# A decoder trunk's opening and closing: gains carried by the first activation tile, casts in transfer order, first unit by tiles, last add in halves

## The chip, the core and the metric

One core of a Trainium2 chip runs the kernel alone. The metric is the device time of one execution in microseconds. A kernel's time is the median of several executions; beside it stands one profiled execution with its own time, whose trace gives the rows shown here. TensorE multiplies matrices, VectorE (DVE) and ScalarE (ACT) do elementwise work, GpSimd (POOL) does some more of it, and SyncE (SP) issues most transfers. Each of these has a queue of instructions that it works through in order.

## The reference

Two decoder layers over a residual stream of 256 rows by 2048 columns in float32. Layer 0 uses differential attention, layer 1 latent attention; each layer then attends into 256 memory rows and applies a squared-ReLU MLP of 8192 hidden columns. Every step is normed first, and one norm closes the trunk.

```python
def rms_norm(x, g):
    xf = x.astype(jnp.float32)
    y = xf * lax.rsqrt(jnp.mean(xf * xf, axis=-1, keepdims=True) + EPS)
    return (y * g.astype(jnp.float32)).astype(x.dtype)
...
    for i in range(DEPTH):
        h = rms_norm(x, attn_norm[i])
        x = x + attention(h)            # differential, then latent
        x = x + memory_cross_attention(rms_norm(x, cross_norm[i]), mem_h, ...)
        x = x + sq_relu_mlp(rms_norm(x, mlp_norm[i]), mlp_wup[i], mlp_wdown[i])
    return rms_norm(x, final_norm)
```

(The attention branches are drawn together into one call here.)

## The kernel before, in words

**Products in three passes.** TensorE works on numbers split in two: a value is cast to a short form (the high half), and what is lost by that is kept as a second number (the low half). A product of activation and weight is high x high, high x low and low x high, three matmuls of 512 columns each. So every weight tile is first cast by ScalarE (`whi`, line 193) and the rest is taken by VectorE (`wlo`, line 194). Activations that come from memory are split in `given_unit`: ScalarE multiplies a tile by its gain column (line 315), VectorE makes the low half (line 316).

**Units.** A *unit* is 512 rows of the inner dimension, four tiles of 128 (`k` = 0 to 3). Its weights for a chunk of 512 output columns are 128 x 2048 numbers, 1024 KB, in a buffer of the pool `wraw`, of which there are seven (`RAWS`); the activations of a unit as they arrive take such a buffer too. A buffer is given out again once its last reader is done. The halves of the weights lie in `whalf`, two tiles of the four for each unit. `matmul_chunk` runs over the four units of a chunk; for each unit over two halves of the weights (`h`), and in each half it goes through both row tiles (`t` = 0, 1, of 128 rows): `unit_part` then does two tiles `k` with three matmuls each. So a unit is 2 x 2 x 2 x 3 = 24 matmuls.

**Orders.** TensorE's instructions stay in the order in which the program writes them. The loads are kept in their written order on their queue (`load`, line 165). The order of the other engines' instructions comes from a planner that simulates the program when it is built.

**The opening (lines 903 to 922).** ScalarE's queue issues the first unit's weights in four pieces of 512 columns (one for each `k`), then loads its function table. TensorE runs 13 matmuls on a blank tile (`WARM`, line 913). SP's queue issues activation tile 0, the gain columns of all norms (`g`, 61 KB), tile 1, tiles 2 and 3 together, and then for units 1 and 2 the activations in two loads and the weights in two loads, for unit 3 the activations. The norm's row factors come later, from `x` itself; they are multiplied in after the products. `gsub` (line 979) is made from `g` for the end of the first attention.

**The closing (lines 1306 to 1328).** In the last chunk the second row tile's products follow the first's (`turns=True`). When a row tile's last 512 columns are done, VectorE adds them to the residual (`add_residual`, line 439), ScalarE squares and sums them (`sum_squares`, line 322), VectorE and GpSimd make the row factor, and ScalarE and VectorE scale the four pieces of 512 columns, which SP sends out in four transfers of 256 KB. The other pieces were added, squared and multiplied by the gain before.

Of the kernel before, what the change touches and what calls it, by code (L numbers as in the profile page):

```python
# [10 lines left out]
F32 = mybir.dt.float32  # L11
# [6 lines left out]
P = 128  # L18
D = 2048
# [4 lines left out]
WARM = 13  # L24
# [21 lines left out]
def trunk(ctx, tc, x, xT, mem, memT, positions, gcols, gfinal, lam_vecs, consts, W, out):  # L46
# [194 lines left out]
    def matmul_chunk(acts, width=CH, turns=False):  # L241
# [60 lines left out]
    def given_unit(src, u, gcol, pieces=None):  # L302


        dst = Held(unit())
        rows = raw_tile().rearrange("p (k t) -> p k t", t=S)
        for k, n in ((0, 1), (1, 1), (2, 2)) if pieces else ((0, 2), (2, 2)):
            load(rows[:, k : k + n], src[:, 4 * u + k : 4 * u + k + n, :])
            if pieces and k == 0:
                load(g, gcols)  # L310
            for i in range(k, k + n):
                if pieces:
                    pieces.next()
                raw, hi, gain = rows[:, i], dst[:, 0, i], g[:, gcol + 4 * u + i : gcol + 4 * u + i + 1]
                nc.scalar.activation(hi, raw, AF.Copy, scale=gain)  # L315
                nc.vector.scalar_tensor_tensor(dst[:, 1, i], raw, gain, f32(hi), ALU.mult, ALU.subtract)
        return dst

# [583 lines left out]

    first = raw_tile()
    for i in range(4):
        load(first[:, i * CH : (i + 1) * CH], W["da_wqkv"][0][:, i * CH : (i + 1) * CH], nc.scalar)
# [8 lines left out]
    acts = []  # L914
    norm = Stream(G_ATTN)
    pieces = split_pieces(first, 4 * CH, 4)
    ready.append(pieces.halves)
    for u in range(4):
        acts.append(given_unit(xT, u, G_ATTN, pieces if u == 0 else None))
        if 0 < u < 3:  # L920
            ready.append(split_weights(W["da_wqkv"][u], CH, loads=2))
            plan.pop(0)
    posf = keep.tile([P, NT], F32, name="posf")
# [149 lines left out]
    def mlp(l, norm, gnext):  # L1073
# [25 lines left out]
        def finish_chunk(of, ps, nxt):  # L1099
            for t in range(NT):  # L1100
                if of.kind == "up":
                    r = work.tile([P, CH], F32, tag="ev", name=nm("ev"), bufs=EVS)
                    out(*of.halves[0], t, ps[t], r, T_SQ)
                else:
# [203 lines left out]
    ss = [small.tile([P, 4], F32, tag="ss", name=nm("ss"), bufs=6) for _ in range(NT)]  # L1308

    def finish(c, t, ps):  # L1310
        cc = slice(c * CH, (c + 1) * CH)
        sum_squares(ss[t][:, c : c + 1], xs[t][:, cc])
        if c < 3:
            nc.gpsimd.tensor_tensor(xs[t][:, cc], xs[t][:, cc], gf[:, cc], ALU.mult)
            return
        r = row_norm(ss[t], D)
        for i in (3, 0, 1, 2):
            cc = slice(i * CH, (i + 1) * CH)
            y = xs[t][:, cc]
            if i == 3:  # L1320
                nc.vector.scalar_tensor_tensor(y, y, r[:, 0:1], gf[:, cc], ALU.mult, ALU.mult)
            elif i == 2:
                nc.vector.tensor_scalar(y, y, r[:, 0:1], None, ALU.mult)
            else:
                nc.scalar.activation(y, y, AF.Copy, scale=r[:, 0:1])
            nc.sync.dma_start(out[t * P : (t + 1) * P, cc], y)

    down(finish)


# [17 lines left out]
def _layout(i):  # L1348
# [9 lines left out]
    gains = [f["attn_norm"], f["cross_norm"], f["mlp_norm"], f["mem_norm"], f["mla_q_norm"], f["mla_kv_norm"], f["da_subln"]]  # L1358
# [57 lines left out]
```

## Time and profile before

| | |
|---|---|
| median of 3 runs | 2242.32 us (2242.08 to 2243.92) |
| the profiled execution | 2240.69 us |
| its span | 2238.9 us |
| TensorE busy | 2222.1 us, 99% |
| VectorE busy | 1736.5 us, 78% |
| ScalarE busy | 1363.5 us, 61% |
| moved by transfers | 454.72 MB, 203 GB/s over the span |

The span runs from the first to the last event of the trace; the 1.8 us between it and the execution's time lie around it. In a row of the timeline stand the start, the time it took, the engine, the line, the operation, what it writes and reads, the count (xN, where neighbours were drawn together), and in brackets the engine's idle time ahead of it with what ended it. In a table of windows each engine's busy time is followed by the count of its instructions; then come the clock that was granted to TensorE as a share of full speed, the share of the 16 DMA engines that was busy, and GB/s. `SPq` and `ACTq` are the queues' own rows, for the issue of a transfer.

### The profile page before, as it was taken

What the parts mean: (1) busy time and instruction counts of PE and PEld (TensorE: products, weight loads), DVE (VectorE), ACT (ScalarE), POOL (GpSimd) and SP (SyncE); (2) the same over time, 40 slices, a digit from 0 to 9 for tenths busy, and PEclk for the clock granted to TensorE, in tenths of its full rate; (3) what the DMA queues carried; (4) which work ended last, traced back from release to release, by engine and by line L of the source; (5) the groups of instructions that cost most, each with busy time, mean ns of one, the idle gap of its engine ahead of it and who ended that gap; (6) DMA issues with size and microseconds to landing.
All of it is one profiled execution on the core that took longest, in us unless ns stands there. A gap on an engine that the chain in (4) does not pass through costs nothing.

```text
span 2238.9 us, 27408 instructions
## 1 busy us (share of the span) xinstructions
PE 2222.1 (99%) x10521; PEld 1854.8 (83%) x10521; DVE 1736.5 (78%) x1892; ACT 1363.5 (61%) x1815; POOL 129.5 (6%) x222
## 2 busy tenths in 40 slices
PE   9999999999999999999999999999999999999998
PEld 7888888888888888888889888888888888888886
DVE  6655647679889889889865766778988988998974
ACT  6544645666666666666655755566766666665664
POOL 0210110000000000000000311000000000000001
PEclk9999999999999999999999999999999999999999
DMA  9446555435765766775845244634677677677681
GB/s 380 162 144 208 190 194 210 157 132 195 241 216 212 250 220 210 243 223 209 260 169 186 99 142 159 254 132 138 214 255 222 200 255 226 202 249 227 201 281 57
DMA packets 69683, 454.72 MB, mean 203 GB/s; under 512 B 7984, under 2 KB 8368, under 8 KB 17584
## 3 DMA queue, kind: packets, MB, share of 16 engines
q1 hardware_dynamic: 64944, 422.56, 52.4%
q0 software_dynamic: 4032, 29.36, 7.2%
q8 instruction: 82, 1.34, 0.2%
q10 hardware_dynamic: 576, 1.05, 0.2%
q14 instruction: 49, 0.40, 0.0%
HBM read 450.84 MB, written 2.10 MB: 202 GB/s over the span
## 4 chain that ended last, share of the span: by engine, by line
PE 89%; DVE 7%; DMA 2%; issue 1%; ACT 1%; ACTq 0%; POOLq 0%; DVEq 0%
PE mm L155 62%; PE pr L155 21%; DVE wlo L194 4%; PE ax L155 3%; PE ax L159 2%; DMA raw<-in_mlp_wup_dram 1%; PE mm L159 1%; DVE raw L748 1%; DVE unit L386 1%; ACT whi L193 0%; DVE raw L413 0%; DVE x L439 0%; DVE p L800 0%; DMA raw<-in_da_wqkv_dram 0%; DVE raw L397 0%
## 5 line engine op out<-in xcount | busy, mean ns | idle before, releaser
L193 ACT CAST whi<-raw 128x1024 fp32r<-128x1024 f32 (+2 forms) x962 | 1001.5, 1042 | 731.8 <-PE mm L155 593.6
L155 PE MATMUL mm<-whi,unit 128*128 128x512 f32 (+3 forms) x4544 | 1439.1, 389 | 2.3 <-ACT unit L315 1.3
L194 DVE TENSOR_TENSOR wlo<-raw,whi 128x1024 fp32r<-128x1024 f32 (+2 forms) x962 | 1145.0, 1209 | 371.2 <-ACT whi L193 359.5
L155 PEld LDWEIGHTS mm<-whi,unit 128*128 128x128 f32 x4544 | 849.8, 188 | 169.3 <-ACT unit L315 2.5
L155 PE MATMUL mm<-wlo,unit 128*128 128x512 f32 (+3 forms) x2272 | 876.4, 386 | 1.5 <-DVE wlo L194 1.5
L155 PE MATMUL pr<-whi,unit 128*128 128x512 f32 x1568 | 505.6, 391 | 0.0
L155 PEld LDWEIGHTS mm<-wlo,unit 128*128 128x128 f32 x2272 | 427.7, 188 | 81.7 <-DVE wlo L194 2.7
L155 PEld LDWEIGHTS pr<-whi,unit 128*128 128x128 f32 x1568 | 294.4, 188 | 60.8
L155 PE MATMUL pr<-wlo,unit 128*128 128x512 f32 x784 | 305.9, 390 | 1.7 <-DVE wlo L194 1.4
L748 DVE TENSOR_TENSOR raw<-raw,raw 128x2048 f32<-128x2048 f32 x84 | 192.1, 2287 | 33.8 <-DMA raw<-in_mlp_wup_dram 33.5
L155 PEld LDWEIGHTS pr<-wlo,unit 128*128 128x128 f32 x784 | 147.3, 188 | 34.1 <-DVE wlo L194 4.2
L439 DVE TENSOR_TENSOR x<-x,mm 128x512 f32<-128x512 f32 x152 | 100.8, 680 | 17.8 <-PE mm L155 17.3
L740 POOL DMA_DIRECT2D raw<-in_mlp_wup_dram x28 | 24.8, 885 | 1104.7 <-DVE wlo L194 1060.1
L288 ACT CAST unit<-ax 128x512 fp32r<-128x512 f32 (+1 forms) x88 | 48.8, 566 | 28.7 <-PE ax L159 26.2
L328 POOL TENSOR_TENSOR rs<-rs,mhalf 128x1 f32<-128x1 f32 (+1 forms) x28 | 23.6, 846 | 700.0 <-DVE rs L327 700.0
L289 DVE TENSOR_TENSOR unit<-ax,unit 128x512 fp32r<-128x512 f32 (+1 forms) x88 | 57.2, 658 | 3.2 <-ACT unit L288 2.4
L501 ACT ACTIVATE p<-ax,nmax 128x256 f32<-128x256 f32 (+1 forms) x80 | 33.7, 429 | 30.0 <-DVE nmax L499 29.4
L800 DVE TENSOR_TENSOR p<-pr,p 128x512 f32<-128x512 f32 x70 | 47.7, 682 | 0.8 <-PE pr L155 0.8
L1089 ACT ACTIVATE p<-p,r 128x512 f32<-128x512 f32 x56 | 40.5, 723 | 11.2 <-DVE p L800 10.8
L159 PE MATMUL ax<-identr,p 128*128 128x128 f32 x304 | 45.5, 272 | 0.0
L159 PEld LDWEIGHTS ax<-identr,p 128*128 128x128 f32 x304 | 37.4, 139 | 9.3
L322 ACT ACTIVATE junk<-x 128x512 bf16<-128x512 f32 x56 | 35.2, 628 | 9.4 <-DVE x L439 8.4
(135 smaller groups left out, 913.6 us busy)
## 6 DMA issues: line engine op xcount, KB each, us to landing
raw<-in_mlp_wup_dram SPq DMA_DIRECT2D x128, 1024.0 KB, 5.0
raw<-in_mlp_wdown_dram SPq DMA_DIRECT2D x128, 1024.0 KB, 5.1
raw<-in_da_wqkv_dram SPq DMA_DIRECT2D x45, 1024.0 KB, 5.1
raw<-in_mlp_wup_dram POOLq DMA_DIRECT2D x28, 1024.0 KB, 8.8
raw<-in_da_wo_dram SPq DMA_DIRECT2D x16, 1024.0 KB, 4.9
raw<-in_ca_wkv_dram SPq DMA_DIRECT2D x16, 1024.0 KB, 5.0
raw<-in_mla_wo_dram SPq DMA_DIRECT2D x16, 1024.0 KB, 5.9
raw<-in_ca_wq_dram SPq DMA_DIRECT2D x8, 1024.0 KB, 6.4
```

Source lines behind the costliest of these rows:

```text
L155: return nc.tensor.matmul(o, stationary, moving, start=start, stop=stop)
L159: nc.tensor.transpose(o, src, ident)
L193: nc.scalar.copy(hi, r)
L194: nc.vector.tensor_tensor(lo, r, f32(hi), ALU.subtract)
L288: nc.scalar.copy(hi, src)
L289: nc.vector.tensor_tensor(dst[:, 1, :n, t * P : (t + 1) * P], src, f32(hi), ALU.subtract)
L322: nc.scalar.activation(junk[:, : src.shape[1]], src, AF.Square, accum_out=acc)
L439: nc.vector.tensor_tensor(xc, xc, ps, ALU.add)
L501: nc.scalar.activation(pr[:, i * w : (i + 1) * w], sb[:, i * w : (i + 1) * w], AF.Exp, bias=nmax[:, i : i + 1], accum_out=ssum[:, i : i + 1],)
L748: nc.vector.tensor_tensor(o, o, q, ALU.add)
L800: nc.vector.tensor_tensor(o, p, q, op)
L1089: nc.scalar.activation(r, src, AF.Relu, scale=rstd[t])
```

## The change

- **Gains with the first tile.** A new input `xT0` holds the 16 gain columns of the first norm and activation tile 0 side by side. It goes into a buffer `ahead` of the pool `wraw`, which then takes the other three tiles of unit 0 too; units 1 to 3 read their gains from it (`first_gain`). The load of all gains `g` moves from second place on SP's queue to behind unit 1's loads.
- **Transfers.** ScalarE's queue issues weight pieces 0 and 1 only; pieces 2 and 3 go to SP's queue behind tiles 0 and 1, and tiles 2 and 3 follow them. For units 1 and 2 each half of the weights is now loaded ahead of the activations that go with it.
- **Casts in written order.** ScalarE and VectorE keep the written order through the opening: for unit 0 piece and tile in turn, for units 1 and 2 two tiles, then half of the weights.
- **First unit by tiles.** In the first chunk unit 0 takes each `k` through both row tiles before the next `k`. 13 blank matmuls become 9.
- **Closing.** The last piece of a row tile is added and squared in halves of 256 columns, with five partial sums in place of four. The sum is scaled in place. The pieces go out in the order 3, 0, 2, 1, piece 1 from ScalarE's queue.

```diff
-WARM = 13
+WARM = 9
...
+                if by_k and u == 0:
+                    for k in range(2):
+                        at = slice(k * width, (k + 1) * width)
+                        for t in range(NT):
+                            ah, al = acts[0].get(0, 2 * h + k, t), acts[0].get(1, 2 * h + k, t)
+                            mm3(ps[t][:, :width], ah, al, hi[:, at], lo[:, at], h + k == 0, False)
+                    continue
...
-    def given_unit(src, u, gcol, pieces=None):
+    def given_unit(src, u, gcol, gains=None, loads=(), between=None):
...
+        for k in (0, 2):
+            if loads:
+                loads.pop(0)()
+            load(rows[:, k : k + 2], src[:, 4 * u + k : 4 * u + k + 2, :])
+        for k in range(4):
+            given_tile(dst, k, rows[:, k], gains(4 * u + k))
+            if between and k % 2:
+                between()
         return dst
+
+    def given_tile(dst, k, raw, gain):
+        hi = dst[:, 0, k]
+        nc.scalar.activation(hi, raw, AF.Copy, scale=gain)
+        nc.vector.scalar_tensor_tensor(dst[:, 1, k], raw, gain, f32(hi), ALU.mult, ALU.subtract)
...
+    ahead = raw_tile()
     first = raw_tile()
...
+    load_first(0, nc.scalar)
+    load(ahead[:, : 16 + S], xT0)
+    load_first(1, nc.scalar)
+    rows = ahead[:, 16 : 16 + 4 * S].rearrange("p (k t) -> p k t", t=S)
+    load(rows[:, 1], xT[:, 1, :])
+    load_first(2, nc.sync)
+    load_first(3, nc.sync)
+    load(rows[:, 2:], xT[:, 2:4, :])
...
+    acts = [Held(unit())]
+    with tc.manual_schedule(engines={mybir.EngineType.Activation, mybir.EngineType.DVE}):
+        pieces = split_pieces(first, 4 * CH, 4)
+        ready.append(pieces.halves)
+        for k in range(4):
+            pieces.next()
+            given_tile(acts[0], k, rows[:, k], first_gain(k))
+        for u in range(1, 4):
+            if u == 3:
+                acts.append(given_unit(xT, u, G_ATTN, first_gain))
+                continue
+            raw = raw_tile()
+            pieces = split_pieces(raw, 4 * CH, 2)
+            ready.append(pieces.halves)
             plan.pop(0)
+            acts.append(
+                given_unit(
+                    xT, u, G_ATTN, first_gain,
+                    [lambda u=u, raw=raw, at=at: load(raw[:, at], W["da_wqkv"][u][:, at]) for at in (slice(0, 2 * CH), slice(2 * CH, 4 * CH))],
+                    pieces.next,
+                )
+            )
+            if u == 1:
+                load(g, gcols)
...
-            ps = matmul_chunk(acts)
+            ps = matmul_chunk(acts, by_k=gi == i == 0)
...
+    def add_last(t, c, ps):
+
+        for h in range(2):
+            at = slice(h * S, (h + 1) * S)
+            xc = xs[t][:, c * CH : (c + 1) * CH][:, at]
+            nc.vector.tensor_tensor(xc, xc, ps[:, at], ALU.add)
+            sum_squares(ss[t][:, c + h : c + h + 1], xc)
+        tot = small.tile([P, 1], F32, tag="tot", name=nm("tot"))
+        nc.vector.tensor_reduce(tot, ss[t], AX.X, ALU.add)
+        nc.vector.tensor_scalar(tot, tot, 1.0 / D, EPS, ALU.mult, ALU.add)
+        nc.gpsimd.tensor_tensor(tot, tot, mhalf, ALU.pow)
+        for i in (3, 0, 2, 1):
+            cc = slice(i * CH, (i + 1) * CH)
+            y = xs[t][:, cc]
+            if i == 3:
+                nc.vector.scalar_tensor_tensor(y, y, tot, gf[:, cc], ALU.mult, ALU.mult)
+            elif i == 2:
+                nc.vector.tensor_scalar(y, y, tot, None, ALU.mult)
+            else:
+                nc.scalar.activation(y, y, AF.Copy, scale=tot)
+            (nc.scalar if i == 1 else nc.sync).dma_start(out[t * P : (t + 1) * P, cc], y)
...
+    a["xT0"] = np.ascontiguousarray(np.concatenate([f["attn_norm"][0].reshape(16, P).T, a["xT"][:, 0]], axis=1))
```

More of the change, by code (lines that the diff above doesn't have):

```diff
@@ L300, in transpose4 @@
         return pt.rearrange("p (k t) -> p k t", k=4)
-    def given_unit(src, u, gcol, pieces=None):
+    def given_unit(src, u, gcol, gains=None, loads=(), between=None):
         dst = Held(unit())
+        gains = gains or (lambda i: g[:, gcol + i : gcol + i + 1])
         rows = raw_tile().rearrange("p (k t) -> p k t", t=S)
[L307 to L316, printed above, removed]
-        return dst
+        for k in (0, 2):
[6 more added lines that the diff above has]
+                between()
+        return dst
+    def given_tile(dst, k, raw, gain):
+        hi = dst[:, 0, k]
+        nc.scalar.activation(hi, raw, AF.Copy, scale=gain)
+        nc.vector.scalar_tensor_tensor(dst[:, 1, k], raw, gain, f32(hi), ALU.mult, ALU.subtract)
     def sum_squares(acc, src):
@@ L1312, in finish @@
         sum_squares(ss[t][:, c : c + 1], xs[t][:, cc])
[L1313 to L1326, printed above, removed]
+        nc.gpsimd.tensor_tensor(xs[t][:, cc], xs[t][:, cc], gf[:, cc], ALU.mult)
+    finish.last = add_last
     down(finish)
```

24 lines of the change are left out of this document (11 added, 13 removed).

## The prediction

> **What bounds the kernel now.** I read the totals of the page first.
>
> ```profile
> span 2238.9 us, 27408 instructions
> PE 2222.1 (99%) x10521; PEld 1854.8 (83%) x10521; DVE 1736.5 (78%) x1892; ACT 1363.5 (61%) x1815; POOL 129.5 (6%) x222
> ```
>
> TensorE works through 99% of the span, and the change gives it four dummy products less and no other work. So only two places can move the end: the stretch before TensorE runs without a break, and what follows its last product. The chain of waits shows the second.
>
> ```profile
> 2214.93 15.20 PE mm L155 x67
> ...
> 2230.16 0.70 DVE x L439
> ...
> 2230.94 0.73 ACT junk L322 x2
> ```
>
> 67 products in 15.20 us are 0.227 us for each product of 512 columns at full clock. After the last one the end of the second row tile is a chain of single steps. The timeline of TensorE shows the first place.
>
> ```profile
> 1.23 5.61 PE L913 MATMUL ax<-blank 128*128 128x512 bf16 x13 [1.23 <-DVE blank L910]
> 6.93 0.50 PE L155 MATMUL mm<-whi,unit 128*128 128x512 f32 x1
> ...
> 9.47 0.50 PE L155 MATMUL mm<-whi,unit 128*128 128x512 f32 x1 [1.33 <-ACT unit L315]
> ...
> 13.85 0.39 PE L155 MATMUL mm<-whi,unit 128*128 128x512 f32 x1
> ```
>
> The row at 13.85 is the 15th real product, and from there on they follow at 0.227. I measure an opening by one number, its **virtual start**: the time at which product 1 would have begun, had all run at full rate. Before, that is 13.85 - 14 x 0.227 = 10.67 us. Every microsecond by which it moves is a microsecond of the end, as the rest is a full TensorE.
>
> What is late there stands in the rows of ScalarE and VectorE.
>
> ```profile
> 4.26 0.62 ACT L193 CAST whi<-raw 128x512 fp32r<-128x512 f32 x1
> 5.85 0.62 ACT L193 CAST whi<-raw 128x512 fp32r<-128x512 f32 x1 [0.97 <-DMA raw<-in_da_wqkv_dram]
> 6.38 0.50 ACT L315 ACTIVATE unit<-raw,g 128x256 fp32r<-128x256 f32 x1
> ...
> 9.52 0.62 ACT L193 CAST whi<-raw 128x512 fp32r<-128x512 f32 x1
> 10.05 2.50 ACT L315 ACTIVATE unit<-raw,g 128x256 fp32r<-128x256 f32 x6
> 12.45 1.99 ACT L193 CAST whi<-raw 128x1024 fp32r<-128x1024 f32 x2
> ```
>
> ```profile
> 5.34 0.24 DVE L979 TENSOR_SCALAR gsub<-g 128x2 f32<-128x2 f32 x2 [4.16 <-DMA g<-in_gcols_dram]
> 5.49 0.68 DVE L194 TENSOR_TENSOR wlo<-raw,whi 128x512 fp32r<-128x512 f32 x1
> ...
> 10.79 2.46 DVE L316 SCALAR_TENSOR_TENSOR unit<-raw,g,unit 128x256 fp32r<-128x256 f32 x6
> 13.52 2.36 DVE L194 TENSOR_TENSOR wlo<-raw,whi 128x1024 fp32r<-128x1024 f32 x2 [0.28 <-ACT whi L193]
> ```
>
> ScalarE cast weight piece 0 at 4.26, then waited for piece 1 (5.85) before it scaled activation tile 0 (6.38): the order was wrong, as that tile could have been scaled at 4.8. VectorE waited 4.16 us for the gains, for a pair of instructions that nobody needed yet. The last view is the transfers.
>
> ```profile
> 0.00:4.00 4.00, 2.77 (x7) 1.04 (x8) 0.34 (x3) 1.36 (x2) 0.20 (x4) 1.00 0.47 128
> 4.00:8.00 4.00, 3.91 (x10) 1.24 (x8) 1.92 (x5) 1.77 (x4) 0.00 (x0) 1.00 0.92 265
> 8.00:12.00 4.00, 2.67 (x7) 1.79 (x7) 2.91 (x7) 3.50 (x8) 0.00 (x0) 0.75 1.01 389
> 12.00:16.00 4.00, 4.00 (x16) 3.16 (x15) 3.72 (x7) 4.00 (x9) 0.00 (x0) 0.82 1.03 407
> ...
> 2234.40:2237.10 2.70, 0.00 (x0) 0.00 (x0) 0.00 (x0) 0.00 (x0) 0.00 (x0) 0.50 1.03 375
> ```
>
> ```profile
> raw<-in_da_wqkv_dram ACTq DMA_DIRECT2D x1, 256.0 KB, 3.5
> raw<-in_xT_dram SPq DMA_DIRECT2D x1, 128.0 KB, 3.1
> ```
>
> ```profile
> 0.74 1.86 ACTq L165 DMA_DIRECT2D raw<-in_da_wqkv_dram  x4
> 0.75 0.39 SPq L165 DMA_DIRECT2D raw<-in_xT_dram  x1
> ```
>
> In the first of these the columns after the busy times are granted clock, DMA share and GB/s; the second has the first transfer of each queue with its time from issue to landing, the third their issues. From 4 us on the transfers are busy without a pause, at 265 GB/s and later near 400: the opening is bound by bytes, and ScalarE waits for them. The clock column holds a second loss: means of 0.75 over 8 to 12 and 0.82 over 12 to 16 are 2.0 + 1.4 = 3.4 us at half rate (10.0 to 13.4, if it is one piece), up to 1.7 us of work.
>
> **The change, part by part.** *First products.* Weight piece 0 and tile 0 are still issued first, on two queues, at 0.74 and 0.75 us; 3.5 and 3.1 later, at 4.2 and 3.9, both have landed. The gains ride in tile 0 (8 KB more). Then cast to 4.88, scaling (pipelined behind it by 0.53, as 5.85 to 6.38) 4.79 to 5.29, and the first product at 5.35 instead of 6.93. The dummies, 5.61/13 = 0.43 each, end at 1.23 + 9 x 0.43 = 5.1, so they no longer stand in its way. VectorE's two lows follow without the wait for the gains (5.6, 6.0). Gain at this point 1.6 us, but it counts only as far as nothing later is late.
>
> *Unit 0.* What must land is 4 x 256 + 2 x 128 + 8 + 256 = 1544 KB. With the rates of before, 0.51 MB are in at 4.0 and 1.57 MB at 8.0; landing follows the bytes by something between 0 and the 1.8 us that lie between the closing transfers' last bytes (2237.1) and the span's end, and I take 0.7. So the last tile pair lands at 8.7, where before the fourth weight piece was cast from 9.52. The 61 KB of gains and unit 1's activations no longer mix with it. Program order then costs something: scaling of tile 2 stands ahead of the cast of piece 3, although its transfer comes behind it on SP's queue. Tile 2 8.75 to 9.25, cast to 9.8, tile 3 to 10.2, lows to 10.9. Product 19 begins near 10.7; with six products a tile, unit 0 is through at 12.1.
>
> *Unit 1 is late next.* SP now issues 512 KB of its weights ahead of 256 KB of its activations. At 389 GB/s after 8.0 these are in at 9.35 and 10.0, landed at 10.05 and 10.7. ScalarE scales two tiles (2.50/6 = 0.42 each) to 11.6 and casts 1024 columns (1.05) to 12.65; VectorE's low part (2.36/2, 1.2) ends at 13.9. Product 25 can start at 12.7, product 26 needs the low part: 13.95. **Virtual start: 13.95 - 25 x 0.227 = 8.28**, a gain of 2.4 us. Behind it nothing is late: the second half lands at 12.1, its low is ready at 15.9, and product 37 is due at 16.45; unit 2's halves are ready at 17.9 and 19.9, due at 19.2 and 21.9. The bounds: with 407 GB/s from 5.2 us on the same sum gives 7.3; with landing 1.8 instead of 0.7 behind the bytes it gives 9.4. The gains, now issued behind unit 1, are needed at the earliest by the instructions at 5.34 above; if these again stand in VectorE's queue ahead of a low part, they cost from 0 to the 0.6 us by which they held it before (4.9 to 5.49).
>
> *The clock.* TensorE now pauses near 8.5 to 9.3 and 12.1 to 13.9. The row at 9.47 has a pause of 1.33 us, and half clock came by 10.0. By that row another stretch may follow here; where it falls into the waiting it costs nothing, behind 13.95 up to 1.7. I take nothing: the stretch of before is in its 10.67, and the pauses now are spread between more products. [...]
>
> *Closing.* The add of 512 columns and its square become two of 256.
>
> ```profile
> L515 DVE TENSOR_TENSOR raw<-ax,raw 128x256 fp32r<-128x256 f32 x12 | 5.0, 417 | 0.3 <-ACT raw L514 0.3
> ```
>
> ```profile
> L322 ACT ACTIVATE junk<-x x56: 620/629/633, 30.9 to 2230.9; 128x512 bf16<-128x512 f32 x56
> ...
> L322 ACT ACTIVATE junk<-ax x16: 362/384/385, 96.4 to 378.5; 128x256 bf16<-128x256 f32 x16
> ```
>
> Before: 2230.16 + 0.70 + 0.08 + 0.73 = 2231.67. After: add 0.42, the same 0.08, then two squares of 0.73 - 0.245 = 0.48 with their read: 2231.62. The second add hides under the first square. Gain 0.05, bounds -0.1 (0.1 of latency between the halves) and 0.25 (the reads overlap). The 1 MB of output still leaves at 375 GB/s, 2.8 us; its first piece is ready no sooner, so moving one of four issues to ScalarE's queue and exchanging two is worth 0 to 0.1. The first row tile's closing lies under the second's products.
>
> *The rest.* TensorE's order is written by hand and stays; that of ScalarE and VectorE behind the opening is planned anew. Of TensorE's idle 2238.9 - 2222.1 = 16.8 us, 1.2 and 1.3 lie in the opening and 8.8 behind 2230.1; the 5.5 left are what a new order could add to or take from. I take 0, bounds 1 either way.
>
> **Sum:** 2.4 + 0.05. The profiled execution took 2240.69 us (span 2238.9 and 1.8 around it); it would take 2238.2. The three runs shown have a median 1.63 us above it, so the forecast is 2242.32 - 2.45 = 2239.9.
>
> **The rivals.**
> *A second half-clock stretch* behind the pause at 12.1 to 13.9. For it speaks the row at 9.47, against it that more of that window is filled with products. Price: up to 1.7, on average some 1.3; 2241.2.
>
> *The opening moves more.* If the transfers reach 407 GB/s as soon as the two single tiles are through, the virtual start is 7.3 (gain 3.4); and the runs shown may have lost to the half clock what the profiled one did not (1.63 above it). Together 5.1; 2237.2. Against it: 265 GB/s over four microseconds in which two queues were full.
>
> *Slower: the first buffer is held.* The gains lie in the first activation tile, so its buffer is free only when unit 3 is scaled, by my sum near 21.4, not 11. If unit 3's weights take that buffer, their transfer starts then.
>
> ```profile
> raw<-in_da_wqkv_dram SPq DMA_DIRECT2D x45, 1024.0 KB, 5.1
> ```
>
> Landed 26.5, cast and low 2.3, 28.8, for product 74: virtual start 28.8 - 73 x 0.227 = 12.2, plus up to 1.7 of half clock after so long a pause: 2244 to 2245.5. It decides once that transfer is issued after about 19.8. Against it: the first weight buffer comes free near 10.5 and would be taken first; the held one only leaves one buffer fewer to run ahead with.
>
> *It doesn't do what it says:* unit 1 was the bound anyway and the transfers come no sooner; then the gain is under 1 us and the time 2241.5. I count this with the first rival.
>
> **How the numbers follow.** Forecast 0.50 (its own range 2238.9 to 2241.0), second stretch or little gain 0.22, more gain 0.20, held buffer 0.08. A measurement of this kernel tells about 0.2%, 4.5 us, from no change: faster means below 2237.8, slower above 2246.8. Faster: most of the third case, 0.20. Slower: the end of the held buffer, if x and the tables come late too, 0.05. Within: 0.75. The range goes from the third case's price to a little short of the held buffer's: 2236.9 to 2243.6.
>
> **What would show it.** Right: first real product near 5.35, product 26 at 13 to 14, VectorE's gains instructions behind unit 0, a virtual start near 8.3, the add to the total 1.45 us. Wrong: a pause of TensorE after unit 2 (held buffer), half clock behind 14 us (second stretch), or a wait in the body that was not there.

## The result, and the profile after

The changed kernel is slower, by 0.16%: its median is 2244.68 us (22 executions, 2242.95 to 2248.09) against 2241.09 us for the kernel before, run on the same chip (22 executions); ratio 1.0016, 95% interval 1.0010 to 1.0023. The profiled executions are 2242.95 and 2240.69 us, spans 2240.9 and 2238.9.

The opening itself did what was forecast. The timeline of TensorE in the changed kernel:

```profile
5.99 0.51 PE L155 MATMUL mm<-whi,unit 128*128 128x512 f32 x1 [1.26 <-ACT unit L328]
...
12.30 0.51 PE L155 MATMUL mm<-whi,unit 128*128 128x512 f32 x1 [0.31 <-ACT whi L193]
13.56 0.51 PE L155 MATMUL mm<-wlo,unit 128*128 128x512 f32 x1 [0.76 <-DVE wlo L194]
13.91 0.63 PE L155 MATMUL mm<-whi,unit 128*128 128x512 f32 x2
```

Product 26 starts at 13.56 and product 27 at 13.91, and from there on they follow at 0.227. The virtual start is 13.91 - 26 x 0.227 = 8.0 us; before it was 10.67. The windows of the changed kernel (after the busy times: granted clock, DMA share, GB/s) show the clock at 1.00 through the opening, where the kernel before had 0.75 and 0.82:

```profile
0.00:4.00 4.00, 2.77 (x7) 1.03 (x8) 0.34 (x3) 1.49 (x2) 0.20 (x4) 1.00 0.45 100
4.00:8.00 4.00, 2.74 (x11) 1.52 (x9) 2.17 (x5) 2.57 (x5) 0.00 (x0) 1.00 1.02 368
...
12.00:16.00 4.00, 2.94 (x12) 2.20 (x13) 3.72 (x8) 3.56 (x7) 0.00 (x0) 1.00 1.04 400
```

So 2.67 us were won by 14 us, in this pair of profiles. They were gone by 64 us. The waits of TensorE between 14 and 120 us, in the same kernel:

```profile
PE mm L159 <- POOL ev L472: 2.6, 2, 2.1
PE mm L155 <- DVE wlo L194: 0.8, 1, 0.8
```

The second of these is the one at 13.56. The first is new; the kernel before has no wait at all in this stretch. Its rows in the timeline of TensorE, first in the changed kernel:

```profile
59.49 0.39 PE L155 MATMUL mm<-whi,unit 128*128 128x512 f32 x1
60.41 0.66 PE L159 MATMUL mm<-identr,ev 128*128 128x128 f32 x4 [0.53 <-POOL ev L472]
63.17 0.66 PE L159 MATMUL mm<-identr,ev 128*128 128x128 f32 x4 [2.11 <-POOL ev L472]
63.59 0.47 PE L155 MATMUL mm<-whi,unit 128*128 128x512 f32 x1
```

and in the kernel before:

```profile
62.17 0.39 PE L155 MATMUL mm<-whi,unit 128*128 128x512 f32 x1
62.41 1.03 PE L159 MATMUL mm<-identr,ev 128*128 128x128 f32 x8
63.20 0.47 PE L155 MATMUL mm<-whi,unit 128*128 128x512 f32 x1
```

These are the transposes of the first q (two row tiles, four transposes each), placed at a fixed point in TensorE's written order. From the product ahead of them to the product behind them it is 63.59 - 59.49 = 4.10 us, before 63.20 - 62.17 = 1.03: **3.07 us lost where 2.67 had been won**, +0.40. At the same masked product behind it the two kernels stand at 80.93 and 80.53, the same +0.40.

What the transposes wait for is the rotation of q by position. ScalarE scales the product by the row norm (`evacuate`, line 456; 444 before), makes the sine and cosine tables (lines 1008 and 1012; 963 and 967), and GpSimd rotates the tile in six small operations (lines 467 to 472; 455 to 460). ScalarE in the kernel before:

```profile
51.72 1.05 ACT L193 CAST whi<-raw 128x1024 fp32r<-128x1024 f32 x1 [1.29 <-PE mm L155]
52.67 0.68 ACT L444 ACTIVATE ev<-mm,rq 128x512 f32<-128x512 f32 x1
53.38 1.28 ACT L963 ACT_TABLE_LOAD   x1
54.67 0.28 ACT L963 ACTIVATE sin<-ang 128x96 f32<-128x96 f32 x1
...
56.95 0.28 ACT L967 ACTIVATE cos<-ang 128x96 f32<-128x96 f32 x1
```

and in the changed kernel:

```profile
51.76 1.06 ACT L193 CAST whi<-raw 128x1024 fp32r<-128x1024 f32 x1 [1.57 <-PE mm L155]
52.72 0.68 ACT L456 ACTIVATE ev<-mm,rq 128x512 f32<-128x512 f32 x1
53.30 1.25 ACT L456 ACTIVATE ev<-mm,r 128x512 f32<-128x512 f32 x2
54.57 1.28 ACT L1008 ACT_TABLE_LOAD   x1
55.86 0.28 ACT L1008 ACTIVATE sin<-ang 128x96 f32<-128x96 f32 x1
...
56.99 0.28 ACT L1012 ACTIVATE cos<-ang 128x96 f32<-128x96 f32 x1
```

The last rotation of the second q tile, in the timeline of GpSimd, before

```profile
61.22 1.30 POOL L460 TENSOR_TENSOR ev<-rope,rope 128x64 f32<-128x64 f32 x1
```

and in the changed kernel

```profile
62.80 0.32 POOL L472 TENSOR_TENSOR ev<-rope,rope 128x64 f32<-128x64 f32 x1
```

ended at 62.52 and 63.12. TensorE needs it for its fifth transpose, before at about 62.8 (62.41 plus half of the 0.79 to 63.20). So before this chain was ready 0.3 us ahead of its use; after, TensorE comes 2.7 us sooner and the chain 0.6 us later. Two things are to be seen in ScalarE's rows. The clock times hardly differ, but measured in products they do: the cast at 51.72 stands (51.72 - 10.67) / 0.227 = 181 products behind the virtual start, the one at 51.76 stands 193 behind it. The chain was put one weight cast, 12 products or 2.72 us, later in ScalarE's queue: counted in the traces, 22 weight casts stand ahead of the sine, before 21. And k's two evacuations (`ev<-mm,r`) now stand ahead of the table load.

The closing gained next to nothing, as forecast. Two rows of VectorE at the end of the changed kernel's timeline:

```profile
2232.25 0.75 DVE L1362 TENSOR_TENSOR x<-x,mm 128x256 f32<-128x256 f32 x2 [1.67 <-PE mm L155]
...
2233.79 0.16 DVE L1365 TENSOR_REDUCE tot<-ssf 128x1 f32<-128x5 f32 x1 [0.79 <-ACT junk L334]
```

From the add to the total it is 1.54 us, before 1.53; from the add to the span's end 2240.9 - 2232.25 = 8.65, before 2238.9 - 2230.16 = 8.74.

Between 81 us and the last add the changed kernel lost another 1.7 us (2232.25 - 80.93 against 2230.16 - 80.53). The first experiment shows what that is.

### The profile page after: what moved, and what is told of

Its sections match the earlier page's. It is cut to its first block, busy times and chain, and to the rows that moved or that the text cites. A ratio compares the mean times of both kernels' runs of the same rounds, so it can differ in the third digit from the quotient of the medians.

```text
span 2240.9 us, 27401 instructions
## 1 busy us (share of the span) xinstructions
PE 2219.8 (99%) x10517; PEld 1852.4 (83%) x10517; DVE 1735.9 (77%) x1894; ACT 1363.3 (61%) x1819; POOL 128.7 (6%) x222
## 4 chain that ended last, share of the span: by engine, by line
PE 86%; DVE 8%; DMA 2%; issue 2%; ACT 1%; POOL 0%; POOLq 0%; DVEq 0%; ACTq 0%
PE mm L155 60%; PE pr L155 20%; DVE wlo L194 5%; PE ax L155 3%; PE ax L159 2%; DMA raw<-in_mlp_wup_dram 2%; DVE raw L760 1%; PE mm L159 1%; ACT whi L193 1%; DVE unit L398 1%; DVE raw L425 0%; DVE p L812 0%; DVE x L451 0%; DMA raw<-in_xT_dram 0%; DVE unit L297 0%
## 5 line engine op out<-in xcount | busy, mean ns | idle before, releaser
L334 ACT ACTIVATE junk<-x 128x512 bf16<-128x512 f32 (+1 forms) x58 | 35.6, 614 | 8.9 <-DVE x L1362 5.5
```

The source lines that it names most:

```text
L334: nc.scalar.activation(junk[:, : src.shape[1]], src, AF.Square, accum_out=acc)
```

## The experiments

All runs are compared with the kernel before on the same chip in the same sitting. Since the time of an execution scatters by some 2 us, each profile is also read at a **mark**: the first product of the first MLP that waits for VectorE, near 530 us; it has the same wait of 0.57 us in every trace. The table has the new wait, the mark, the stretch from the mark to the last add, and how many executions had a mean granted clock below 0.999. In the first profile of before, with one stretch of 3.41 us at half clock, that mean is 0.998, in the first of the changed kernel, with none among its products, 0.999; runs 6, 9, 11 and 12, with half clock, have 0.998, and 4 and 13, at full clock in the windows read, 0.999. By the same count the kernel before was below 0.999 in 49 of its 109 executions beside the runs.

| run | wait for the rotated q, us | mark, us | mark to last add, us | median, before, us | ratio (95%) | clock below 0.999 |
|---|---|---|---|---|---|---|
| before, first profile | 0 | 529.62 | 1700.54 | | | |
| changed, first profile | 2.6 | 530.10 | 1702.15 | 2244.68, 2241.09 | 1.0016 (1.0010 to 1.0023) | 14 of 22 |
| 1 closing only | 0 | 530.44 | 1702.24 | 2243.23, 2243.66 | 1.0001 (0.9992 to 1.0010) | 5 of 11 |
| 2 opening only | 2.6 | 531.61 | 1704.26 | 2246.42, 2243.66 | 1.0010 (1.0001 to 1.0019) | 9 of 11 |
| 3 later transposes | 0 | 529.16 | 1705.06 | 2243.21, 2243.66 | 0.9998 (0.9989 to 1.0007) | 0 of 11 |
| 4 early tables | 0 | 527.12 | 1705.33 | 2242.85, 2243.66 | 0.9992 (0.9983 to 1.0001) | 0 of 11 |
| 5 before, early tables | 0 | 527.98 | 1703.62 | 2241.72, 2243.49 | 0.9996 (0.9987 to 1.0005) | 5 of 11 |
| 6 before, slow rotation | 3.3 | 533.62 | 1702.54 | 2247.08, 2243.49 | 1.0019 (1.0010 to 1.0027) | 8 of 11 |
| 7 = 4, unit 0 by halves | 0 | 527.02 | 1703.89 | 2242.14, 2243.49 | 0.9995 (0.9986 to 1.0003) | 3 of 11 |
| 8 = 4, planned casts | 0 | 526.04 | 1702.47 | 2240.67, 2243.49 | 0.9987 (0.9978 to 0.9996) | 0 of 11 |
| 9 changed, planned casts | 2.6 | 530.15 | 1705.17 | 2245.18, 2243.77 | 1.0004 (0.9995 to 1.0014) | 9 of 11 |
| 10 = 8, all gains early | 0 | 526.71 | 1704.85 | 2240.85, 2243.77 | 0.9987 (0.9978 to 0.9996) | 0 of 11 |
| 11 changed, again | 2.6 | 531.57 | 1702.57 | 2245.48, 2243.77 | 1.0007 (0.9998 to 1.0016) | 9 of 11 |
| 12 changed, x sooner | 3.8 | 534.22 | 1703.47 | 2248.20, 2241.70 | 1.0026 (1.0016 to 1.0037) | 7 of 7 |
| 13 changed, k behind tables | 0.7 | 527.81 | 1701.93 | 2241.30, 2241.70 | 0.9999 (0.9990 to 1.0008) | 0 of 11 |

**1: the closing alone.**

```diff
 (before, with add_last, five partial sums, pieces out in the order 3, 0, 2, 1)
+                elif of.c == 3 and hasattr(nxt, "last"):
+                    nxt.last(t, of.c, ps[t])
```

> The kernel before with the closing edits alone (last piece added and squared in halves, new order of the four pieces out). My theory, that the opening's gain is eaten at 60 us by TensorE's wait for GpSimd's rotation of the first q and that the closing is worth almost nothing: within 0.5 us of the kernel before, ratio 0.9995 to 1.0003, add of the last 512 columns to the span's end 8.6 to 8.7 us. Rival, that the closing or what is planned anew for it costs the 1.7 us that appear behind 81 us: 1 to 2 us slower, ratio 1.0005 to 1.0009, with the loss behind 835 us of the trace.

Ratio 1.0001, and from the add (2232.68) to the end of its span of 2241.4 it is 8.7 us: the closing is worth nothing that can be measured. This run also settles the 1.7 us. Up to the closing its ScalarE, VectorE and GpSimd work through the same operations in the same order as in the kernel before. The mark in the first profile of before, in the timeline of TensorE:

```profile
529.62 0.50 PE L155 MATMUL pr<-wlo,unit 128*128 128x512 f32 x1 [0.57 <-DVE wlo L194]
```

and the mark and the last add in this run:

```profile
530.44 0.50 PE L155 MATMUL pr<-wlo,unit 128*128 128x512 f32 x1 [0.57 <-DVE wlo L194]
...
2232.68 0.75 DVE L1317 TENSOR_TENSOR x<-x,mm 128x256 f32<-128x256 f32 x2 [1.67 <-PE mm L155]
```

The body took 2230.16 - 529.62 = 1700.54 us there and 1702.24 here. Over all profiles it lies between 1700.5 and 1705.3, whatever was changed ahead of it, and the first profile of before has the shortest. Part of the difference is TensorE waiting for the low halves of weights: 2.9 us in the first profile of before, 3.5 in this run, 5.6 in run 4; what makes up the rest was not found. Run 6, whose ScalarE and VectorE keep the order of before from end to end, has 1702.54, more than the changed kernel's 1702.15: the 1.7 us are scatter, not the change.

**2: the opening alone.**

```diff
 (changed kernel, with finish() and row_norm of before; no add_last)
```

> The changed kernel with the closing of before. My theory: as the whole change, 2 to 3.6 us slower than before, ratio 1.0010 to 1.0017, with TensorE's wait of about 2.6 us for GpSimd's ev at 60 to 63 us. Rival, the closing is to blame: at or below the kernel before, ratio 0.9990 to 1.0003.

The same wait of 2.6 us and 2.8 us above before: the loss is the opening's. The mean clock of this profile is 0.998, and 9 of its 11 executions had the lower clock; the mark lies 1.5 us behind that of the changed kernel's first profile.

**3: later transposes.**

```diff
-            yield T_ROT + (10.0 if given else 0.0) if rot else T_EV
+            yield T_ROT + (14.0 if given else 0.0) if rot else T_EV
```

> The changed kernel with the first heads' transposes placed 4 us later in TensorE's written order, so that other products stand where it waited. My theory: no wait of TensorE for ev near 60 us, the offset to before at 81 us goes from +0.4 to -1.9 or less, and the time falls by 2.0 to 2.7 us against the changed kernel: ratio to before 0.9993 to 1.0006. Rival, the wait only moves (to the k heads, or to the attention that needs them): offset at 81 us stays above -0.5, ratio 1.0010 or more. Rival, the loss lies in the half clock or in the body planned anew: the wait goes but the time stays at 1.0010 to 1.0020.

The wait is gone and so is the half clock (0 of 11), and the time falls to 0.9998. But the mark is only 0.9 us ahead of the changed kernel's. The offset at 81 us can't be read here, since the masked product was written later as well. The 4 us shift what follows, and TensorE waits in another place, at the end of the fourth attention group:

```profile
370.38 0.74 PE L155 MATMUL ax<-unit,raw 128*128 128x256 f32 x4 [1.05 <-DVE raw L527]
374.45 0.63 PE L159 MATMUL ax<-identr,os 128*128 128x128 f32 x4 [1.75 <-DVE os L671]
```

In the kernel before that place has one wait of 0.36, in the changed kernel one of 0.4. So 2.4 us of the 3.1 came back as another wait: my first rival, in a place that I had not named.

**4: early tables.**

```diff
-    hooks[1] = lambda: load(const, consts)
-    hooks[2] = lambda: x_pieces(0, 1)
+    def first_loads():
+        load(const, consts)
+        load(pos, positions)
+
+    def tables_early():
+        x_pieces(0, 1)
+        tables()              # sine and cosine only; the lambdas stay late
...
+    hooks[1] = first_loads
+    hooks[2] = tables_early
```

> The changed kernel with the sine and cosine tables made some 30 us earlier (positions loaded behind the constants, tables ahead of the norm of x), so that GpSimd's rotation waits only for the evacuated q. My theory, that the chain behind the tables is what TensorE waits for: the second q tile is rotated by 58 us, no wait for ev near 60 us, the time 2.0 to 2.7 us below the changed kernel, ratio to before 0.9993 to 1.0006. Rival, the chain is held by the norm of x and the evacuation, not by the tables: the wait stays above 1.5 us, ratio 1.0008 or more. Rival, the earlier tables delay casts in the opening: TensorE waits for whi or wlo between 14 and 40 us.

No wait, no half clock in 11 executions, mark at 527.12, 3.0 us ahead of the changed kernel's; the ratio of 0.9992 is just outside what I had written (0.9993 to 1.0006). In the timeline of GpSimd the rotation begins as soon as q is evacuated:

```profile
52.88 0.32 POOL L467 TENSOR_TENSOR rope<-ev,cos 128x64 f32<-128x64 f32 x1 [2.89 <-ACT ev L456]
...
55.47 0.32 POOL L472 TENSOR_TENSOR ev<-rope,rope 128x64 f32<-128x64 f32 x1
```

The second q tile is ready at 55.79, not 63.12. Norm and evacuation are no obstacle; the tables were.

**5: early tables in the kernel before.** The same edit.

> The kernel before with the early sine and cosine tables of the fourth run, nothing else. My theory, that before TensorE came to the first transposes after the rotated tile was ready (62.41 against 62.52, so no wait): nothing to gain, ratio 0.9995 to 1.0004, rotated tile ready 4 us sooner without use. Rival, the early tables are worth something by themselves (their 3 us in the fourth run are then not the wait's): ratio below 0.9992.

0.9996, within scatter of 1: the tables are worth their 3 us only where TensorE waits for them. This run shows something else. Its opening, that of before, began thus:

```profile
6.79 0.50 PE L155 MATMUL mm<-whi,unit 128*128 128x512 f32 x1 [1.21 <-ACT unit L315]
...
14.60 0.50 PE L155 MATMUL mm<-wlo,unit 128*128 128x512 f32 x1 [0.69 <-DVE wlo L194]
14.94 0.62 PE L155 MATMUL mm<-whi,unit 128*128 128x512 f32 x2
```

Product 27 at 14.94 is a virtual start of 9.0; the mean clock was 0.999. By the same sum the three other profiles with the opening of before give 10.7, 10.9 (run 6) and 11.5 (run 1), with a mean clock of 0.998 each. The eight profiles with the written casts of the change (the first, 2, 3, 4, 7, 11, 12 and 13) lie between 7.9 and 8.2.

**6: a slower rotation in the kernel before.**

```diff
+        for _ in range(slow.pop() if slow else 0):      # 8 for the first tile, then 0
+            e.tensor_tensor(m[0], a, c, ALU.mult)
         e.tensor_tensor(m[0], a, c, ALU.mult)
```

> The kernel before with eight more GpSimd products (the same value written again) ahead of the rotation of the first q tile: about 8 x 0.28 = 2.2 us, 1 us more for each that falls beside a subtract of VectorE. My theory, that this chain had about 0.3 us of slack before: TensorE waits 1.9 us or more for ev at 62 us, the time rises by that, with a half-clock stretch behind it in a part of the executions by up to 1.7 more: ratio 1.0006 to 1.0018. Rival, the chain had slack of 2 us or more and something else brought the wait with the new opening: no wait for ev, ratio 0.9996 to 1.0004.

```profile
65.40 0.66 PE L159 MATMUL mm<-identr,ev 128*128 128x128 f32 x4 [2.62 <-POOL ev L463]
66.75 0.66 PE L159 MATMUL mm<-identr,ev 128*128 128x128 f32 x4 [0.69 <-POOL ev L464]
```

Eight operations of some 0.28 us, one of them slow (they are told of below), become 3.3 us of waiting and a ratio of 1.0019, a shade above the range that I had written. No half clock followed this wait in the profile (1.00 in the windows from 60 to 72 us); its stretch lies in the opening (0.73 over 8 to 12, 0.84 over 12 to 16). The chain had no slack of 2 us in the kernel before; it was there all the time, just short of being seen.

**7: unit 0 by halves.** (With the early tables of run 4, as are 8 and 10.)

```diff
-            ps = matmul_chunk(acts, by_k=gi == i == 0)
+            ps = matmul_chunk(acts, by_k=False)
```

> The changed kernel with early tables, and unit 0 multiplied by halves as before (both tiles k for a row tile, then the other row tile). Theory of the prediction, that six products a tile keep TensorE fed: product 4 waits for tile 1, some 1.5 to 2 us of waiting more inside unit 0, but unit 1 is the bound, so the virtual start moves by less than 0.5 us against the 8.1 of the fourth run; a half-clock stretch may come with the longer pause. Ratio 0.9985 to 1.0003. Rival, the order by tiles carries the gain: virtual start 9.5 or later, ratio 1.0002 or more.

Product 27 starts at 13.89, virtual start 8.0; the mark is within 0.1 us of run 4's. The expected wait inside unit 0 didn't show either: tile 1 was there in time. The order by tiles carries nothing that these profiles show. Three of 11 executions had the lower clock, where run 4 had none; whether the order has to do with that is open.

**8: planned casts.**

```diff
-    with tc.manual_schedule(engines={mybir.EngineType.Activation, mybir.EngineType.DVE}):
+    if True:
```

> The changed kernel with early tables, and the order of the opening's casts left to the planner (for unit 0 it puts weight pieces 2 and 3 ahead of tiles 2 and 3). Theory, that transfers and not casts bound the opening: virtual start 7.6 to 8.6 as in the fourth run, ratio 0.9985 to 1.0003. Rival, the written order of the casts carries the gain: virtual start 9.5 or later, ratio 1.0002 or more.

The virtual start is earlier than either theory gave. TensorE runs through unit 1 without the two waits at 12.30 and 13.56; a row there:

```profile
11.62 0.62 PE L155 MATMUL mm<-whi,unit 128*128 128x512 f32 x2
```

Product 21 at 11.62 is a virtual start of 11.62 - 20 x 0.227 = 7.1. Mark 526.04, ratio 0.9987 (0.9978 to 0.9996): the written order of the casts costs the change 1 us, and with the wait and this order gone the kernel is faster than the kernel before, by 0.13%.

**9: planned casts, late tables.** The edit of run 8 in the changed kernel itself.

> The changed kernel with the opening's casts left to the planner, the tables late as in the change. The eighth run's virtual start of 7.1 is 1 us earlier than the changed kernel's 8.0. My theory, that the rotated tile at 63 us is a floor for TensorE: the earlier opening is worth nothing, the wait for ev grows by the same 1 us to 3.2 to 3.8 us in all, and the time is that of the changed kernel within its scatter, ratio to before 1.0008 to 1.0022. Rival, the microsecond comes through: ratio below 1.0006, wait no longer than 2.8 us.

The time can't decide (1.0004 beside 1.0007 for run 11), the trace can, and against my theory. TensorE reached the transposes 1.4 us sooner than in run 11, and the wait is again

```profile
PE mm L159 <- POOL ev L472: 2.6, 2, 2.1
```

since the chain came sooner by as much: sine at 54.45 in place of 55.86 (changed kernel's first profile). The mark is 1.4 us ahead of run 11's, and both have half clock behind the wait (mean clock 0.87 over 60 to 64 us and 0.71 over 64 to 68 here, 0.95 and 0.63 there). **So 63 us is no floor**: the chain moves with TensorE. Its instructions stand in ScalarE's and VectorE's queues between weight casts, and a cast waits until TensorE has freed a buffer (1.57 us ahead of the row at 51.76, with TensorE as the releaser).

**10: all gains early.**

```diff
     load(ahead[:, : 16 + S], xT0)
+    load(g, gcols)
...
-            if u == 1:
-                load(g, gcols)
```

> The eighth run's kernel (early tables, planned casts) with all norms' gains loaded second on SyncE's queue again, as before the change; unit 0 still takes its gains from the first tile's transfer. Theory of the prediction, that these 61 KB and VectorE's pair of instructions for them stand in the way: virtual start 0.2 to 1 us later than 7.1, ratio 0.9985 to 1.0002. Rival, the place of this transfer is worth nothing: virtual start within 0.2 us of 7.1.

Product 30 starts at 14.24, virtual start 7.7, 0.6 us later than in run 8, and the mark is 0.7 later. That fits the theory, but it is one profile each, and the virtual starts of runs 8 and 9, both with planned casts and late gains, differ by 0.5 (7.1 and 6.6). In the median of the executions it is not to be seen. So a cost of the 61 KB is not shown.

**11: the changed kernel again.**

> The changed kernel itself beside the other two on the same chip. My theory: ratio to before 1.0008 to 1.0022, wait for ev of 2.4 to 2.9 us, granted clock lower in about half of the executions. The body between 177 and 2086 us, 1907.5 us in the first profile of before and 1909.1 in the first of the changed kernel, lies here between 1907 and 1913, as in all runs so far: its 1.7 us were scatter. Rival, the body of the changed kernel is really longer than in the runs with its closing and its orders: above 1913.

Wait 2.6, body 1702.57, ratio 1.0007, a shade below what I had written, and half clock in more executions than I had expected. The profile has it too (windows, granted clock third from the end):

```profile
60.16:63.57 3.41, 1.08 (x9) 0.85 (x9) 1.83 (x2) 1.40 (x2) 3.33 (x9) 1.00 0.86 291
63.57:66.98 3.41, 3.41 (x11) 2.73 (x9) 0.69 (x1) 0.59 (x1) 2.94 (x11) 0.50 0.04 17
```

The mark lies 1.5 us behind that of the first profile, where the same pause was followed by full clock. Over the 22 executions of the first sitting the median is 2243.84 us at a mean clock of 0.999 (8 of them) and 2245.89 at 0.998 (11).

**12: x one unit sooner.**

```diff
-    hooks[2] = lambda: x_pieces(0, 1)
...
-    hooks[6] = first_norm
+    hooks[1] = first_loads            # constants and the first piece of x
+    hooks[2] = lambda: x_pieces(1, 1)
...
+    hooks[5] = first_norm
```

> The changed kernel with the loads and squares of x, its norm and the tables issued one unit of products sooner (constants and first piece together). The ninth run has felled the fixed time of 63 us: there the whole chain came 1.4 us sooner with TensorE, and the wait stayed 2.6. New theory: the chain's instructions stand in the in-order queues of ScalarE and VectorE between weight casts that wait for TensorE, and in the changed kernel's plan the tables stand one cast (2.72 us of products) later than in the plan of before; here ScalarE's queue has nine casts ahead of the sine again, not ten. So sine near 52 to 53 us, second q tile rotated by 60.5, wait for ev at most 0.6 us, ratio to before 0.9985 to 1.0002. Rival, the transfers of x hold the chain: the squares wait for x, the wait stays above 1.5 us, ratio 1.0006 or more.

A miss. The chain did come 4.1 us sooner: sine at 52.17, in the timeline of ScalarE right behind the evacuation and the table load, and the second q tile ready at 59.01.

```profile
50.18 0.68 ACT L456 ACTIVATE ev<-mm,rq 128x512 f32<-128x512 f32 x1
50.88 1.28 ACT L1008 ACT_TABLE_LOAD   x1
52.17 0.28 ACT L1008 ACTIVATE sin<-ang 128x96 f32<-128x96 f32 x1
```

But the transposes came 5.3 us sooner (wait from 54.62 on; 59.88 in the changed kernel): their place in the written order is counted from the point at which the norm is issued, and I had moved that point. The wait grew to 3.8 us, with half clock in the profile (mean clock 0.77 over 56 to 60 us, 0.50 over 60 to 64). The run still answers its question about the transfers: no square waited for x.

**13: k's evacuations behind the tables.**

```diff
+            if given and dst is behind:                       # k of the first group
+                with tc.issue_after(last_table[0].ins):       # the cosine
+                    e = evacuate(ps, scale())
+            else:
+                e = evacuate(ps, scale() if given else scale)
```

> The changed kernel with k's two evacuations put behind the cosine in ScalarE's queue, nothing else. New theory (place in the queue): the table load starts at 53.3 in place of 54.57, sine 1.2 us sooner, second q tile rotated at 61.6 to 62.2 in place of 63.12, wait 1.2 to 1.8 us in place of 2.6; time between the changed kernel and the early tables: ratio 0.9995 to 1.0012. Rival, the k evacuations only fill a hole and cosine or GpSimd are late for another reason: second tile within 0.3 us of 63.1, wait 2.4 us or more.

Two instructions of ScalarE change places with the tables, and nothing else. ScalarE:

```profile
52.59 0.68 ACT L456 ACTIVATE ev<-mm,rq 128x512 f32<-128x512 f32 x1
53.29 1.28 ACT L1016 ACT_TABLE_LOAD   x1
54.58 0.28 ACT L1016 ACTIVATE sin<-ang 128x96 f32<-128x96 f32 x1
...
55.71 0.28 ACT L1020 ACTIVATE cos<-ang 128x96 f32<-128x96 f32 x1
```

Sine and cosine come 1.3 us sooner. GpSimd gains more than that, as two of its twelve operations are slowed beside a subtract of VectorE (1.18 and 1.30 us) where three were (1.19, 1.30 and 1.30): the second q tile is ready at 60.86, 2.3 us sooner, and so sooner than I had written. TensorE waits

```profile
PE mm L159 <- POOL ev L472: 0.7, 1, 0.7
```

and no execution of 11 has a clock below 0.999 (14 of 22 and 9 of 11 in the changed kernel). Ratio 0.9999, mark 2.3 us ahead of the changed kernel's. This is the most direct test: with the opening left as it is, and every other instruction of ScalarE, VectorE and GpSimd in its old order, the place of the tables in ScalarE's queue is worth 2.3 of the 3.07 us.

## Why the prediction was wrong, step by step

**The opening, right in its sum.** Forecast 8.28 for the virtual start, measured 8.0 (7.9 to 8.2 in eight profiles). The first product came at 5.99, not 5.35: the first four microseconds moved 100 GB/s where I had carried over 128. Weight piece 0 was cast from 4.91, not 4.26. It cost nothing, as I had said of everything ahead of unit 1: unit 1 was late next, product 26 at 13.56 (forecast 13.95). Runs 2 and 4 bear this out: there unit 0's products followed at 0.43 us, half the rate of 0.227, up to between 9.5 and 10.1 us (the clock column of run 4 says 1.00 there all the same, so the counts of half clock leave this start out), and the virtual start was 8.0 and 8.1. That the program order of the casts costs something is shown by run 8 (1 us); that the gains' transfer does is not shown (run 10). That products by tiles matter was wrong by the profile of run 7, though the sum didn't rest on it. VectorE's gains pair stood behind unit 0, at 13.43, and held nothing back that TensorE waited for.

**The closing, right that it is worth next to nothing.** Forecast gain 0.05 us, measured 0.09 from the add to the span's end. But the step that was to bring it did not: from the add to the total I had put 1.45 us, and it is 1.54, before 1.53. So the 0.09 lie behind the total, where I had put 0 to 0.1.

**The rivals.** No pause after unit 2, so the held first buffer cost nothing. The half-clock stretch was priced well (1.7 us; 1.5 at the mark between two profiles of the changed kernel, 2.05 between the medians) but expected behind 14 us. It came behind the pause at 60 us. The slower outcome came by a mechanism that was not among the rivals; only the last sign of being wrong, "a wait in the body that was not there", named it.

**The step that failed** is "The rest": "that of ScalarE and VectorE behind the opening is planned anew", and "I take 0, bounds 1 either way". It measured 3.07 us in the profiled pair, with another 1.5 to 2 of half clock in more than half of the executions (14 of 22). With it fell the sentence on which the sum stood, "Every microsecond by which it moves is a microsecond of the end, as the rest is a full TensorE". A full TensorE says that nothing is late at the old pace; it doesn't say by how much the next thing was early. The row for that stood in the trace of before, in GpSimd's timeline: the second q tile ended at 62.52, needed at 62.8. I had looked for what is late behind the opening up to unit 2 only. My bound came from the idle time that TensorE had (5.5 us spread over the body), and that is no bound on what an order made anew can add.

My first explanation after the result, a chain fixed at 63 us that eats any gain, was also wrong: run 9 moved it. What holds by runs 4, 9, 12 and 13 is that the chain's place in ScalarE's queue makes it late: counted in casts that TensorE paces it was one cast later, and it had k's evacuations ahead of the tables. Why the planner placed it so for the new opening was not tried.

**Of the size.** 2.67 won less 3.07 lost is 0.4 us at 81 us, or some 2 with the half clock. The 2.67 hang on one profile of before, and so did the 2.4 of the forecast: the opening of before, in the same order each time, started at 9.0 without the stretch of half clock (run 5) and at 10.7 to 11.5 with it. Against the first the change won 1.0 us, against the last 3.5. With 1.3 us for the half clock (2.05 in 14 of 22 executions), an estimate from these numbers is a loss of 0.9 us (3.07 - 3.5 + 1.3) to 3.4 (3.07 - 1.0 + 1.3). Between the medians it was 1.7 in run 11's sitting and 3.6 in the first, just above. How often the kernel before had its stretch in the first sitting is not on record, so the difference between the two sittings stays open.

## What to carry to other kernels

Before a gain at the front of a full engine is booked at the end, list for each later chain when its result was ready and when it was used, and take the smallest of these slacks as what the gain may cost; here the next one had 0.3 us. Where a planner orders the other engines, a changed opening changes their orders far behind it: compare the positions of side work in the queue, counted in products, not in microseconds. What stands on a side engine between buffer-paced casts should be issued as early as its inputs allow: the tables, early, with the casts left to the planner, gave the fastest versions (runs 8 and 10, 0.9987 of the time before).

## What the runs showed of the hardware

- **Half clock after short pauses.** Granted clock fell to half for 3.4 us at a time after pauses of TensorE of 1.33 us (the kernel before), 1.87 (run 6, opening), 2.24 (run 1, opening) and 0.52 + 2.11 (run 11), but not after 1.21 (run 5), 1.26 (the changed kernel's opening) or 1.35 (run 10, opening), nor after 0.53 + 2.11 in the first profile of the changed kernel or 2.62 in run 6. By runs 11 and 13 the length of the pause counts: with 2.6 us of waiting in the profile 9 of 11 executions had a clock below 0.999, with 0.7 us none of 11.
- **Where the pause falls seems to count too.** In the kernel before the half clock lasted 3.413 us (10.01 to 13.42), and from its end to the fall at 2232.09, behind the last product, it is 650 times as long; in run 11 it lasted as long too (63.57 to 66.98). I call 3.413 us a step and count steps from a change of the clock. In run 11 the pause of 2.11 lay within one step, the first of the two rows shown at run 11 (the second has no idle time); the next step was at half clock. In the changed kernel's first profile the same pause, up to 63.17, was cut by the end of a step at 62.10 (637 steps ahead of the fall at 2236.39, behind the last product), and the clock stayed. So it did in run 6, where by my estimate one near 64.5 cut the pause of 2.62: its half clock ended near 13.3 (0.84 over 12 to 16), and 15 steps are 51.2 us. The steps in the changed kernel's first profile:

```profile
58.69:62.10 3.41, 1.85 (x10) 1.07 (x8) 1.98 (x2) 1.63 (x2) 3.41 (x7) 1.00 0.51 127
62.10:65.51 3.41, 2.34 (x12) 2.01 (x13) 1.46 (x3) 0.59 (x1) 3.25 (x12) 1.00 0.48 202
```

  In the step ahead of the half clock TensorE idled for 1.42 us in the kernel before (6.60 to 10.01) and for 2.33 in run 11, but for 1.56 in the changed kernel's first profile (58.69 to 62.10), where the clock stayed. In every later step of the kernel before that ends ahead of its last product it idled for at most 0.86. So a step's idle time sorts these nearly but not wholly. If steps decide, whether one program meets the half clock depends on where they lie in an execution. That is my reading of these traces; no run varied it.
- **GpSimd beside VectorE.** A rotation operation of GpSimd on 128x64 mostly took 0.32 us in the first profiles of both kernels, and 1.19 to 1.41 where it began within the first 0.22 us of VectorE's subtract of 1024 columns; the changed kernel's GpSimd, for one:

```profile
57.34 1.19 POOL L467 TENSOR_TENSOR rope<-ev,cos 128x64 f32<-128x64 f32 x1 [0.45 <-ACT cos L1012]
58.49 1.30 POOL L469 TENSOR_TENSOR rope<-ev,cos 128x64 f32<-128x64 f32 x1
```

  VectorE had two of these subtracts from 57.12 to 59.61; the second of the slow operations ends 0.18 us behind them (59.79). Each such overlap makes the chain about 1 us longer (1.30 in place of 0.32).
